# Head copies by the engines instead of DMA, and two-span projections that share one order of passes

## The chip, the cores and the metric

The kernel runs on one core of a Trainium2 chip. The metric is the time of one execution on the device in microseconds (us); lower is better. The time of a version is the median of several executions. A profile is taken from one further execution, which has its own time.

## The reference

A decoder trunk of two layers over 528 positions (16 meta tokens and 512 inputs) of width 1024. Each layer does, cut to what matters here:

```python
proj = h @ w_in[l]                    # 1024 -> 4168 columns
a, g, zc, q, k, v, za, qi, ki, wi = split(proj)
y_conv = silu(layer_norm(causal_conv31(a * sigmoid(g)))) * silu(zc)
q, k, qi, ki = rope(q), rope(k), rope(qi), rope(ki)
score = sum_h relu(qi_h . ki) * wi_h  # 8 index heads, one shared key
keep the 132 best causal keys of each query by score
y_attn = softmax(q . k on kept keys) . v * silu(za)    # 8 heads of 64
h = layer_norm(ALPHA * h + concat(y_conv, y_attn) @ w_out[l])
```

The output is h without the meta tokens. All of it is in float32 accuracy.

## The kernel before

**Layout and arithmetic.** Channels lie on the 128 partitions and positions along the free dimension. A float32 operand of a large product is split into a high part (rounded to the fp32r type, in which TensorE streams fast) and a low part (the rest). A product is then three passes over the 8 tiles of the contraction: high weight by high input, high weight by low input, low weight by high input. The input of a layer is kept as `HI` and `LO` (rows `hh` and `hl` of the profile).

**Projections.** `project(col, lo, evac)` computes one block of 128 output columns. The 528 positions don't fit one PSUM bank, so `spans` cuts them in two column spans, 0 to 272 and 272 to 528; a projection that needs at most 512 positions has one span. That holds for the four `i` jobs of each layer (396 positions, from 132 on) and, in the last layer, for the `z`, `q` and `a` jobs (512 positions, from 16 on). Of the 66 projections 46 have two spans: 29 in the first layer, 17 in the second. `product` writes the 24 matmuls of one span: 16 with the high weights, then 8 with the low weights. The PSUM tiles `acc` of the projections, `acco` of the output products and those of the `v` transposes come from one ring of three buffers (tag `acc`).

**Weights.** `weight` loads a block in two halves. For each half SyncE issues the load into `wraw` (7 buffers), ScalarE makes the high part `whi` (4 buffers) and writes a rounded copy with the opposite sign to `wlo` (5 buffers), to which the weights are then added:

```python
act.activation(h, r, AF.Copy)
act.activation(o, r, AF.Copy, scale=-1.0)
pool.dma_start(o.bitcast(F32), r, accum_op=OP.add)
```

The third line, a DMA issued by GpSimd, leaves the low part in `wlo`. TensorE can start the low pass only when that DMA has landed.

**Heads.** A block of q, k or qi columns holds two heads of 64 channels, one on each half of the partitions. `heads_q` and `heads_k` apply rope and then make one 128-partition operand for each head. For q and qi it holds the high part of the head on its own half and the low part on the other half; for k there are two, with the high part on both halves and with the low part on both halves. What must cross to the other half goes by DMA issued on SyncE. `job_kw` copies the shared index key to both halves in the same way.

**Order of the work.** All operations are recorded first. `Planner` then simulates them with prices (`_price`), latencies (`delay`) and queues, and writes each engine's program in the planned order. `ORDER` is the order of recording, `SHIFT` a table of offsets to the rank of each job, in nanoseconds. Matmuls of one `group` share one rank. The planner may put matmuls of different jobs between each other; matmuls that add into one PSUM bank stay in the order of recording. `delay` holds the planner's latency of a DMA: for one issued by GpSimd it adds 650 ns to the issue cost and the transfer. The chip's engines execute the result strictly in that order and wait on semaphores where data are late.

**Elsewhere.** `convolve` is 31 multiply-adds on VectorE for each of four channel blocks, `score` computes index scores and finds the 132 best by repeated max and replace on VectorE, `attend` does the attention, `mix` the output projection with `product` over 4 tiles, and `norm` the layer norms. Job names are those of `ORDER`: `u` (a and g), `i` (qi), `kw`, `z`, `q`, `k`, `v`, `a` (za), `s12` and `s34` (scores), `c01` and `c23` (convolution), `cl` (its layer norm), `t` (attention), `o` and `oa` (output).

Of the kernel before, what the change touches and what calls it, by code (L numbers as in the profile page):

```python
# [8 lines left out]
F32 = mybir.dt.float32  # L9
F32R = mybir.dt.float32r  # L10
BF = mybir.dt.bfloat16
AF = mybir.ActivationFunctionType
OP = mybir.AluOpType

P = 128
D = 1024
KT = D // P
# [16 lines left out]
C_KW = 32  # L34
# [10 lines left out]
)  # L45
SHIFT = {
# [21 lines left out]
}  # L68
W1 = NM + P
K_COS = 0  # L70
# [14 lines left out]
class Planner:  # L85
# [84 lines left out]

    def delay(self, a, b, true):
        if a.dma:
            far = 650.0 if a.eng == "pool" else 1950.0
            return far + a.tail + (900.0 if b.eng == "sp" else 1067.0 if b.eng == "pe" else 950.0)
        if a.eng == b.eng and (not true or a.eng == "pe"):
            return 0.0
        return self.LAT.get((a.eng, b.eng), 120) + (200.0 if (a.eng, b.eng, a.tail) == ("dve", "act", 1)
                                                    else 0.0)
# [161 lines left out]
def tile_hymba(ctx: ExitStack, tc: tile.TileContext, xt: bass.AP, wi: bass.AP, wv: bass.AP,  # L340
# [3 lines left out]
    pe, act, dve, pool, sync = (pl.engine(e) for e in ("pe", "act", "dve", "pool", "sp"))  # L344
    T = pl.tile
# [5 lines left out]
    ps = ctx.enter_context(tc.tile_pool(name="ps", bufs=1, space=bass.MemoryType.PSUM))  # L351

    HI = T(cp, [P, KT, L], F32R, name="hh")
    LO = T(cp, [P, KT, L], F32R, name="hl")
# [37 lines left out]
                w.extend(t[:, n, :] if len(t.shape) == 3 else t[:, n // 2, n % 2, :] for n in range(step))  # L392
        return W

    def product(acc, w, hi, lo, kt=KT):
        n = 0
        pl.group = len(pl.ops) + 1
        for s, m in ((w[0], hi), (w[0], lo), (w[1], hi)):
            for k in range(kt):
                pe.matmul(acc, s[k], m(k), start=(n == 0), stop=(n == 3 * kt - 1))  # L400
                n += 1
        pl.group = 0

    mean_1 = T(cp, [P, 2], F32, name="mean_c")
# [4 lines left out]
    for _ in range(SPIN):  # L409
        pe.matmul(spin[:, :2 * P], mean_c[:, 0, :], mean_1[:, 0:1].to_broadcast([P, 2 * P]), start=True,  # L410
                  stop=True)
# [31 lines left out]
    for l in range(DEPTH):  # L443
# [4 lines left out]
        def spans(lo):  # L448
            return [(lo, L)] if L - lo <= 512 else [(max(a, lo), b) for a, b in HALVES]

        def project(col, lo, evac):
            w = weight(wi[l, col], *(fresh.pop(0)() if fresh else (pool,)))
            for a, b in spans(lo):
                acc = T(ps, [P, 512], F32, name="acc", tag="acc", bufs=3)[:, :b - a]
                product(acc, w, lambda k: HI[:, k, a:b], lambda k: LO[:, k, a:b])
                evac(acc, a, b)

        def row(name, dt=F32):
            tag, n = {"xq": ("x", 2), "xk": ("x", 2), "ki": ("x", 2), "vt": ("x", 2), "rot": ("rot", 2),
                      "lq": ("lq", 2), "sg": ("sg", 1)}.get(name, ("rl", ROWS))  # L460
            return T(sp, [P, L], dt, name=name, tag=tag, bufs=n)

        def copy_to(x, scale=1.0):
            return lambda acc, a, b: act.activation(x[:, a:b], acc, AF.Copy, scale=scale)

        def rope(x, a):
            rot = row("rot")
            for g in range(2):
                sync.dma_start(rot[g::2, a:], x[1 - g::2, a:])
            dve.tensor_mul(x[:, a:], x[:, a:], cosT[:, a:])  # L470
            dve.tensor_mul(rot[:, a:], rot[:, a:], sinT[:, a:])
            dve.tensor_add(x[:, a:], x[:, a:], rot[:, a:])

        def split(x, a, hi, lo):
            act.activation(hi[:, a:], x[:, a:], AF.Copy)
            dve.tensor_tensor(lo[:, a:], x[:, a:], hi[:, a:].bitcast(F32), op=OP.subtract)

        def heads_q(col, a, keep, scale=1.0):
            x = row("xq")
            project(col, a, copy_to(x, scale))  # L480
            rope(x, a)
            s0, s1 = keep("s0"), keep("s1")
            lo = row("lq", F32R)
            split(x, a, s0, lo)
            act.activation(s1[64:, a:], x[64:, a:], AF.Copy)
            sync.dma_start(s1[:64, a:].bitcast(F32), lo[64:, a:].bitcast(F32))
            sync.dma_start(s0[64:, a:].bitcast(F32), lo[:64, a:].bitcast(F32))
            return s0, s1

        def heads_k(col, keep):  # L490
            x = row("xk")
            project(col, 0, copy_to(x))
            rope(x, 0)
            s0, s1, l0, l1 = (keep(n) for n in ("k0", "k1", "kl", "km"))
            split(x, 0, s0, l0)
            act.activation(s1[64:, :], x[64:, :], AF.Copy)
            act.activation(l1[64:, :], l0[64:, :], AF.Copy)
            for one, two in ((s0, s1), (l0, l1)):
                sync.dma_start(two[:64, :].bitcast(F32), two[64:, :].bitcast(F32))
                sync.dma_start(one[64:, :].bitcast(F32), one[:64, :].bitcast(F32))  # L500
            return (s0, s1), (l0, l1)

        def dots(qs, ks, kls, q0, m, a, b):
            out = [T(ps, [P, 512], F32, name="pl", tag="s", bufs=2)[:m, :b - a] for _ in range(2)]
# [7 lines left out]
        kw = T(sp, [P, L], F32, name="kw", tag="s01")  # L512
# [6 lines left out]

        def job_kw():  # L520
            ki = row("ki")
            project(C_KW, 0, copy_to(kw))
            for s in (0, 64):
                sync.dma_start(ki[s:s + 64, :], kw[0:64, :])
            rope(ki, 0)
            split(ki, 0, kih, kil)
            po = turn(ki, P)
            act.activation(kihr, po, AF.Copy)
            dve.tensor_tensor(kilr, po, kihr.bitcast(F32), op=OP.subtract)
# [188 lines left out]
        def keep(j):  # L718
            return lambda name: T(sp, [P, L], F32R, name=name, tag=f"{name}{j % 2}")

        def job_q(j):
            ready[j, "q"] = (heads_q(C_Q + j, qlo, keep(j), -HD ** -0.5),)

        def job_k(j):
            ready[j, "k"] = heads_k(C_K + j, keep(j))
# [9 lines left out]
        def chunks(i):  # L735
            a, b = HALVES[i]
            a = max(a, qlo)
            return a, b, [(c, min(P, b - c)) for c in range(a, b, P)]
# [77 lines left out]

        def mix(j, k0, w, hi, lo, a, b):
            acc = T(ps, [P, 512], F32, name="acco", tag="acc", bufs=3)[:, :b - a]
            product(acc, w, lambda k: hi[:, k, a:b], lambda k: lo[:, k, a:b], 4)
            r = R[j // 4][:, j % 4, a:b]  # L820
            dve.scalar_tensor_tensor(r, r, 1.0 if k0 else ALPHA, acc, op0=OP.mult, op1=OP.add)

# [35 lines left out]
        for i in range(2):  # L858
            pl.job = f"ln{i}/{l}"
            a, b, _ = chunks(i)  # L860
            norm(lambda j: R[j // 4][:, j % 4, :], KT, mean_c[:, 0, :], i, V_PG, pool, i == 1)
            for j in range(KT):
# [4 lines left out]
                else:  # L867
# [6 lines left out]
                    if not last and j % 2:  # L874
                        pool.tensor_tensor(LO[:, j, a:b], r, HI[:, j, a:b].bitcast(F32),
                                           op=OP.subtract)
# [68 lines left out]
```

## Time and profile before

| | |
|---|---|
| median of 3 executions | 675.14 us (672.87 to 675.35) |
| the profiled execution | 671.79 us |
| its span, first to last instruction | 669.8 us |
| mean granted TensorE clock, share of full speed | 0.989 |
| busy, share of the span | PE 95%, PEld 89%, DVE 78%, ACT 69%, POOL 29% |

PE are the matmuls of TensorE and PEld its weight loads, which overlap them; DVE is VectorE, ACT ScalarE, POOL GpSimd, SP SyncE, which only issues DMAs here. All instructions of this kernel are issued through one helper and so have one line number; rows are told apart by their tiles, written out<-in. A bracket at the end of a row tells how long the engine was idle before it and what ended that.

### The profile page before, as it was taken

The page shows a single profiled execution, that of the slowest core. Times are in us where ns is not written, and L with a number is a line of the kernel's source. Part 1 is how long each engine was busy: PE and PEld are TensorE (multiplying, and loading weights), DVE is VectorE, ACT ScalarE, POOL GpSimd, SP SyncE. Part 2 cuts the span into 40 slices and gives each one's busy share as a digit, 9 for nine tenths or more (in the row PEclk, how much of TensorE's full clock was granted, in tenths as well). Part 3 has the DMA queues.
Part 4 walks back from the last instruction along what each step waited for, and adds up shares of the span by engine and source line. Part 5 has one row for each costly group of instructions (what it writes and reads, how often), then busy time and mean ns, then how long its engine had stood idle before and what let it go on. Part 6 is the DMA issues. An engine that isn't in the chain of part 4 may idle for free.

```text
span 669.8 us, 13204 instructions
## 1 busy us (share of the span) xinstructions
PE 639.0 (95%) x4602; PEld 598.1 (89%) x4602; DVE 524.0 (78%) x1279; ACT 463.8 (69%) x1056; POOL 191.9 (29%) x236
## 2 busy tenths in 40 slices
PE   8999999999999998899999999999999999989993
PEld 7989999999999987899898999888999889967992
DVE  5686999999899947444563999999999999483356
ACT  7554865865756979596676665667549887895536
POOL 0423213223211322444543232223231121233262
PEclk8999999999999999899999999999999999999997
DMA  8899849748855586998315985887886783279503
GB/s 299 203 263 219 237 95 236 168 98 197 198 131 130 127 224 170 200 212 199 75 68 139 225 212 131 191 212 173 189 186 163 166 188 90 87 177 238 82 1 125
DMA packets 67570, 112.60 MB, mean 168 GB/s; under 512 B 7600, under 2 KB 21168, under 8 KB 67376
## 3 DMA queue, kind: packets, MB, share of 16 engines
q0 software_dynamic: 25088, 41.95, 37.5%
q1 hardware_dynamic: 42416, 69.81, 33.2%
q8 instruction: 36, 0.59, 0.3%
q14 instruction: 30, 0.25, 0.1%
HBM read 50.46 MB, written 4.26 MB: 82 GB/s over the span
## 4 chain that ended last, share of the span: by engine, by line
PE 56%; issue 15%; DMA 9%; DVE 6%; ACT 5%; POOL 2%; SPq 0%; POOLq 0%; ACTq 0%; DVEq 0%
PE acc L297 28%; PE acco L297 11%; DMA wlo<-wraw 5%; PE o L297 5%; PE pl L297 3%; PE pp L297 3%; PE pq L297 2%; POOL wlo L297 2%; DVE r L297 2%; DVE sc L297 1%; DMA s<-lq 1%; PE pm L297 1%; DMA kl<-kl 1%; DMA qi<-lq 1%; DMA rot<-xq 1%
## 5 line engine op out<-in xcount | busy, mean ns | idle before, releaser
L297 POOL DMA_DIRECT2D wlo<-wraw x140 | 124.0, 939 | 350.7 <-ACT wlo L297 214.1
L297 DVE SCALAR_TENSOR_TENSOR conv<-u,vec,conv 128x528 f32<-128x528 f32 (+1 forms) x240 | 176.4, 755 | 1.8
L297 PE MATMUL acc<-hh,whi 128*128 128x272 f32 (+3 forms) x872 | 154.0, 308 | 5.0 <-ACT hh L297 2.5
L297 PE MATMUL acc<-hl,whi 128*128 128x272 f32 (+3 forms) x872 | 148.1, 303 | 0.0
L297 PE MATMUL acc<-hh,wlo 128*128 128x272 f32 (+3 forms) x872 | 144.5, 304 | 3.8 <-DMA wlo<-wraw 3.5
L297 PEld LDWEIGHTS acc<-hh,whi 128*128 128x128 f32 x872 | 125.1, 190 | 11.7 <-ACT hh L297 3.9
L297 PEld LDWEIGHTS acc<-hh,wlo 128*128 128x128 f32 x872 | 123.8, 190 | 10.7 <-DMA wlo<-wraw 6.2
L297 ACT ACTIVATE whi<-wraw 128x512 fp32r<-128x512 f32 (+1 forms) x148 | 86.9, 614 | 66.3 <-PE acc L297 51.1
L297 PEld LDWEIGHTS acc<-hl,whi 128*128 128x128 f32 x872 | 124.6, 190 | 3.9 <-issue 0.2
L297 ACT ACTIVATE wlo<-wraw 128x512 fp32r<-128x512 f32 x140 | 85.5, 623 | 6.9 <-PE acc L297 4.8
L297 DVE SCALAR_TENSOR_TENSOR r<-r,acco 128x256 f32<-128x256 f32 (+2 forms) x56 | 25.8, 462 | 47.4 <-PE acco L297 47.3
L297 DVE MAX8 m<-sc 128x8 f32<-128x400 f32 (+3 forms) x106 | 55.9, 551 | 0.0
L297 DVE MATCH_REPLACE8 sc<-m,sc 128x400 f32<-128x400 f32 (+3 forms) x98 | 53.6, 549 | 0.0
L297 ACT ACTIVATE p<-p,ast 128x400 f32<-128x400 f32 (+4 forms) x72 | 40.6, 568 | 5.0 <-DVE ast L297 4.7
L297 PE MATMUL o<-v,pt 128*128 128x64 f32 x320 | 43.0, 265 | 0.5 <-ACT pt L297 0.4
L297 PEld LDWEIGHTS o<-v,pt 128*128 128x128 f32 x320 | 41.5, 192 | 1.7 <-ACT pt L297 1.1
L297 ACT ACTIVATE rl<-pl 128x272 f32<-128x272 f32 (+3 forms) x80 | 29.5, 391 | 14.8 <-PE pl L297 12.1
L297 DVE CUSTOM_DVE_ANT_0 p<-pl,bmask 128x272 f32<-128x272 f32 (+3 forms) x80 | 33.0, 433 | 7.7 <-PE pl L297 6.2
L297 ACT ACTIVATE pt<-pp 128x128 f32<-128x128 f32 (+3 forms) x64 | 26.9, 433 | 11.5 <-PE pp L297 10.7
L297 ACT ACT_TABLE_LOAD x26 | 33.4, 1283 | 1.5 <-PEq L936 0.7
L297 DVE SCALAR_TENSOR_TENSOR sc<-rl,ws,sc 12x144 f32<-12x144 f32 (+3 forms) x56 | 29.9, 555 | 0.6 <-ACT rl L297 0.3
L297 PE MATMUL pp<-konst,p 128*128 128x128 f32 x160 | 30.2, 289 | 0.0
(167 smaller groups left out, 1067.5 us busy)
## 6 DMA issues: line engine op xcount, KB each, us to landing
wlo<-wraw POOLq DMA_DIRECT2D x140, 256.0 KB, 4.9
wraw<-wi SPq DMA_DIRECT2D x128, 256.0 KB, 3.8
wraw<-wo SPq DMA_DIRECT2D x32, 256.0 KB, 4.1
hl<-wraw POOLq DMA_DIRECT2D x16, 256.0 KB, 5.2
rot<-xk SPq DMA_DIRECT2D x16, 132.0 KB, 2.7
k<-k SPq DMA_DIRECT2D x16, 132.0 KB, 3.1
r<-xt SPq DMA_DIRECT2D x2, 1056.0 KB, 8.9
r<-spill SPq DMA_DIRECT2D x2, 1024.0 KB, 6.2
```

The costliest lines, as they stand in the source:

```text
L297: self.plan.record(self.e, fn, lambda: real(*a, **k), reads, writes, *_price(self.e, fn, named, reads, writes))
```

## The change

Five edits, made together.

1. `heads_q`: for each head, ScalarE copies its 64 partitions to the high part in place, and VectorE subtracts and writes the low part straight to the other 64 partitions. Before, one ScalarE copy and one subtraction covered 128 partitions, one more ScalarE copy 64, and two DMAs moved the low parts.
2. `heads_k`: for each head three more such steps; the four DMAs are gone, and ScalarE writes the copies to the other half.
3. `job_kw`: ScalarE copies the shared index key from PSUM to both halves, instead of two DMAs.
4. `product` takes all spans of a projection at once. High weights by high and low inputs are done for the first span and then for the second, and then the low weights for the first and the second. All are one group. For one span the order is as before, in `mix` too.
5. The planner's price of a GpSimd DMA goes from 650 to 1800 ns, and the `SHIFT` table is another one. `ORDER` is the same.

```diff
 SHIFT = {
-    "a0/1": 301146, "a1/0": -624491, "a1/1": -132089, "a2/0": 1188874, "a2/1": -413625,
+    "a0/0": -21811, "a0/1": 62045, "a1/0": -1672691, "a1/1": -4829, "a2/0": -278500, "a2/1": -2793,
...
     def delay(self, a, b, true):
         if a.dma:
-            far = 650.0 if a.eng == "pool" else 1950.0
+            far = 1800.0 if a.eng == "pool" else 1950.0
...
-    def product(acc, w, hi, lo, kt=KT):
-        n = 0
+    def product(accs, w, hi, lo, spans, kt=KT):
+        count = dict.fromkeys(range(len(accs)), 0)
         pl.group = len(pl.ops) + 1
-        for s, m in ((w[0], hi), (w[0], lo), (w[1], hi)):
-            for k in range(kt):
-                pe.matmul(acc, s[k], m(k), start=(n == 0), stop=(n == 3 * kt - 1))
-                n += 1
+        for ps_ in (((w[0], hi), (w[0], lo)), ((w[1], hi),)):
+            for i, (acc, (a, b)) in enumerate(zip(accs, spans)):
+                for s, m in ps_:
+                    for k in range(kt):
+                        pe.matmul(acc, s[k], m[:, k, a:b], start=(count[i] == 0),
+                                  stop=(count[i] == 3 * kt - 1))
+                        count[i] += 1
         pl.group = 0
...
             w = weight(wi[l, col], *(fresh.pop(0)() if fresh else (pool,)))
-            for a, b in spans(lo):
-                acc = T(ps, [P, 512], F32, name="acc", tag="acc", bufs=3)[:, :b - a]
-                product(acc, w, lambda k: HI[:, k, a:b], lambda k: LO[:, k, a:b])
+            accs = [T(ps, [P, 512], F32, name="acc", tag="acc", bufs=3)[:, :b - a] for a, b in spans(lo)]
+            product(accs, w, HI, LO, spans(lo))
+            for acc, (a, b) in zip(accs, spans(lo)):
                 evac(acc, a, b)
...
-            s0, s1 = keep("s0"), keep("s1")
-            lo = row("lq", F32R)
-            split(x, a, s0, lo)
-            act.activation(s1[64:, a:], x[64:, a:], AF.Copy)
-            sync.dma_start(s1[:64, a:].bitcast(F32), lo[64:, a:].bitcast(F32))
-            sync.dma_start(s0[64:, a:].bitcast(F32), lo[:64, a:].bitcast(F32))
-            return s0, s1
+            ss = keep("s0"), keep("s1")
+            for g, t in enumerate(ss):
+                own, other = x[64 * g:64 * g + 64, a:], slice(64 - 64 * g, 128 - 64 * g)
+                hi = t[64 * g:64 * g + 64, a:]
+                act.activation(hi, own, AF.Copy)
+                dve.tensor_tensor(t[other, a:], own, hi.bitcast(F32), op=OP.subtract)
+            return ss
...
-            s0, s1, l0, l1 = (keep(n) for n in ("k0", "k1", "kl", "km"))
-            split(x, 0, s0, l0)
-            act.activation(s1[64:, :], x[64:, :], AF.Copy)
-            act.activation(l1[64:, :], l0[64:, :], AF.Copy)
-            for one, two in ((s0, s1), (l0, l1)):
-                sync.dma_start(two[:64, :].bitcast(F32), two[64:, :].bitcast(F32))
-                sync.dma_start(one[64:, :].bitcast(F32), one[:64, :].bitcast(F32))
-            return (s0, s1), (l0, l1)
+            hs, ls = [[keep(n) for n in ns] for ns in (("k0", "k1"), ("kl", "km"))]
+            for g, (h, t) in enumerate(zip(hs, ls)):
+                own, other = slice(64 * g, 64 * g + 64), slice(64 - 64 * g, 128 - 64 * g)
+                act.activation(h[own, :], x[own, :], AF.Copy)
+                dve.tensor_tensor(t[own, :], x[own, :], h[own, :].bitcast(F32), op=OP.subtract)
+                act.activation(h[other, :], x[own, :], AF.Copy)
+                act.activation(t[other, :], t[own, :].bitcast(F32), AF.Copy)
+            return hs, ls
...
-            project(C_KW, 0, copy_to(kw))
-            for s in (0, 64):
-                sync.dma_start(ki[s:s + 64, :], kw[0:64, :])
+
+            def evac(acc, a, b):
+                act.activation(kw[:, a:b], acc, AF.Copy)
+                for g in (0, 64):
+                    act.activation(ki[g:g + 64, a:b], acc[:64], AF.Copy)
+            project(C_KW, 0, evac)
...
-            product(acc, w, lambda k: hi[:, k, a:b], lambda k: lo[:, k, a:b], 4)
+            product([acc], w, hi, lo, [(a, b)], 4)
```

## Rows read from the trace of the kernel before

**Rows 1.** The page: busy time of each engine, and the DMA total.

```profile
PE 639.0 (95%) x4602; PEld 598.1 (89%) x4602; DVE 524.0 (78%) x1279; ACT 463.8 (69%) x1056; POOL 191.9 (29%) x236
...
DMA packets 67570, 112.60 MB, mean 168 GB/s; under 512 B 7600, under 2 KB 21168, under 8 KB 67376
```

**Rows 2.** Timeline, second layer: matmuls that follow each other (start, duration).

```profile
393.53 1.11 PE L297 MATMUL acc<-hh,whi 128*128 128x256 f32 x8
...
394.48 1.11 PE L297 MATMUL acc<-hl,whi 128*128 128x256 f32 x8
```

**Rows 3.** Waits of the weight loads: total us, times, longest us.

```profile
PEld acc L297 <- DMA wlo<-wraw: 6.2, 10, 1.4
PEld acco L297 <- DMA wlo<-wraw: 5.7, 2, 4.3
...
PEld pl L297 <- DMA s<-lq: 1.7, 1, 1.7
```

**Rows 4.** Timeline of the weight loads at four of the waits for wlo.

```profile
27.74 0.66 PEld L297 LDWEIGHTS acc<-hh,wlo 128*128 128x128 f32 x4 [0.80 <-DMA wlo<-wraw]
...
103.83 0.81 PEld L297 LDWEIGHTS acc<-hh,wlo 128*128 128x128 f32 x6 [0.33 <-DMA wlo<-wraw]
...
270.11 0.93 PEld L297 LDWEIGHTS acco<-ych,wlo 128*128 128x128 f32 x4 [4.34 <-DMA wlo<-wraw]
...
403.66 0.54 PEld L297 LDWEIGHTS acc<-hh,wlo 128*128 128x128 f32 x4 [1.38 <-DMA wlo<-wraw]
```

**Rows 5.** DMA issues: count, KB each, median us from issue to landing.

```profile
wlo<-wraw POOLq DMA_DIRECT2D x140, 256.0 KB, 4.9
...
k<-k SPq DMA_DIRECT2D x16, 132.0 KB, 3.1
```

**Rows 6.** Waits of the SP queue, whole span: total us, times, longest.

```profile
SPq L297 <- DMA wlo<-wraw: 222.3, 88, 6.6
...
SPq L297 <- ACT k L297: 21.4, 6, 9.5
...
SPq L297 <- DVE lq L297: 15.7, 7, 5.6
```

**Rows 7.** Timeline of the last q block of the second layer.

```profile
600.96 0.68 DVE L297 TENSOR_TENSOR lq<-xq,s 128x512 fp32r<-128x512 f32 x1
...
605.47 3.23 SPq L297 DMA_DIRECT2D s<-lq  x2
...
612.16 0.34 PE L297 MATMUL pl<-k,s 128*128 128x144 f32 x1 [1.26 <-DMA s<-lq]
```

**Rows 8.** ACT and DVE groups by form: busy us, mean ns of one | idle before.

```profile
L297 ACT ACTIVATE k<-xk 128x528 fp32r<-128x528 f32 x8 | 5.1, 643 | 1.5 <-DVE xk L297 1.5
L297 ACT ACTIVATE k<-xk 64x528 fp32r<-64x528 f32 x8 | 5.1, 643 | 0.2
...
L297 ACT ACTIVATE kw<-acc 128x272 f32<-128x272 f32 x2 | 0.8, 386 | 1.6 <-PE acc L297 1.6
...
L297 DVE TENSOR_TENSOR kl<-xk,k 128x528 fp32r<-128x528 f32 x8 | 5.6, 698 | 0.2 <-ACT k L297 0.2
...
L297 DVE TENSOR_TENSOR lq<-xq,qi 128x396 fp32r<-128x396 f32 x8 | 4.6, 570 | 3.9 <-ACT qi L297 3.8
```

**Rows 9.** Windows: busy us and count of PE, PEld, DVE, ACT, POOL; PEclk, DMA share, GB/s.

```profile
0.00:80.00 80.00, 74.78 (x507) 71.04 (x508) 58.47 (x113) 50.10 (x112) 20.61 (x30) 0.98 0.97 250
80.00:240.00 160.00, 157.79 (x1252) 152.36 (x1252) 155.97 (x381) 111.86 (x252) 37.71 (x45) 1.00 0.68 155
...
400.00:560.00 160.00, 158.19 (x1041) 143.25 (x1040) 156.30 (x377) 112.70 (x239) 38.52 (x44) 1.00 0.78 178
```

**Rows 10.** Waits of all engines: ScalarE for a free buffer of high weights.

```profile
ACT whi L297 <- PE acc L297: 51.1, 46, 5.2
```

**Rows 11.** Timeline of VectorE: two instructions of 396 columns in a row.

```profile
401.30 0.55 DVE L297 TENSOR_TENSOR xq<-xq,konst 128x396 f32<-128x396 f32 x1
401.79 0.55 DVE L297 TENSOR_TENSOR rot<-rot,konst 128x396 f32<-128x396 f32 x1
```

41 rows, old and new, of the table SHIFT are left out of this document.

## The prediction

> **What bounds the kernel now.** I read the page first. TensorE is busy for 95% of the span and no other engine for more than 78% [rows 1]. A faster kernel must therefore either give TensorE less work, which this change doesn't (it only reorders the matmuls), or take away times at which TensorE stands still. How dense the stream is when nothing is late is seen in the timeline: eight matmuls of 256 columns start 0.95 us after the eight before them, 0.119 us each [rows 2]. So nearly all of the 669.8 us is a stream that the change leaves as it is, and the prize is small.
>
> The waits of the weight loads show what holds the stream up. The low weights, which a GpSimd DMA finishes, are late ten times before projections (6.2 us) and twice before output products (5.7 us), and a q operand is late once (1.7 us) [rows 3]. That makes 13.6 us, 2.0% of the span, which the change can reach at all. The timeline of the same waits tells which edit reaches them. Five stand before two-span projections, 2.7 us together, the first 0.33 and the last 1.38 [rows 4]. Four, 3.4 us together, the first 0.80, stand before one-span projections, whose order of passes does not change, and the largest of all, 4.34, before an output product [rows 4]. The tenth before projections is some 0.1 us.
>
> Then the two engines that get more work. VectorE has 4.0 us idle between 80 and 240 us and 3.7 us between 400 and 560; ScalarE is at 70% there [rows 9].
>
> **The change, part by part.**
>
> *Low weights last.* In a two-span projection the first low matmul came behind 16 matmuls and now comes behind 32, so 16 × 0.119 = 1.9 us later [rows 2]. The longest of the five waits it concerns is 1.38 [rows 4], so each would be covered. The planner could put matmuls of other work between them before, too, so it doesn't gain more than the waits: -2.5 of the 2.7, bounds 0 and -2.7. The high weights are last read eight matmuls earlier, after 32 of 48 instead of 40, which frees ScalarE's `whi` buffers about 1 us sooner. ScalarE waits 51.1 us for those [rows 10], but it isn't the bound, and I count nothing; the cover is TensorE's own stream.
>
> *Head copies.* Gone are 68 of SyncE's DMAs: 32 for q and qi, 32 for k, 4 for the index key. One takes about 3.1 us to land [rows 5], and before that it waits in an in-order queue which stands on ScalarE's k copies for 21.4 us and on VectorE's `lq` for 15.7 [rows 6]. The last q block shows the whole path: its low part is ready at 601.64, its DMAs are issued from 605.47, and TensorE starts on it at 612.16 [rows 7]. In the new form the subtraction writes the operand itself, about 10 us sooner. TensorE stood still for only 1.7 us of that [rows 3], since output products filled the rest. Taken: -1.7, bounds 0 and -1.7. Behind these DMAs in the queue stand weight loads, but those wait mostly for a buffer, 222.3 us on the low-weight DMAs [rows 6], so I give nothing for loads that can be issued sooner. At most 68 × 132 KB = 9.0 MB of 112.6 MB traffic goes away [rows 1, 5]. Where that could count is the first 80 us, with the DMA engines 97% busy [rows 9]: 8 of the qi copies and 2 of the index key go there, at most 10 × 132 KB = 1.3 MB of 80 × 250 GB/s = 20 MB, 6.6%. If TensorE's idle 5.2 us there (80 less 74.8) were all DMA, that would give it back; taken 0, bounds 0 and -4.
>
> *What the engines get instead.* Half the partitions cost ScalarE the same, 643 ns for 64 or 128 [rows 8]. A q block keeps two copies, a k block goes from three to six: 8 × 3 × 0.643 = 15.4 us. The index key adds four copies in each layer, 8 × 0.386 = 3.1 [rows 8]. ScalarE goes from 463.8 to about 482 us, 72%, behind TensorE's stream: 0. VectorE has one more subtraction in each of 24 blocks, eight of 396 columns and sixteen of about 528: 8 × 0.570 + 16 × 0.698 = 15.7 us [rows 8], 7.9 in each layer. That lands mostly where VectorE has no room [rows 9]. What is late next is the convolution and the selection of keys, which fill that engine, and behind them the convolution's norm and the output products. The cover is attention and projection work that TensorE can take first. Without it the price is the whole 15.7. Of that, 7.7 fits into the idle time of the two full stretches, and the first layer's four qi blocks, 2.3, fall into the first 80 us, where VectorE is idle for 21.5 [rows 9]. Some 5.7 is left, and I let a third of it reach TensorE: +2.0, bounds 0 and +15.7.
>
> One rule speaks against this part. The Trainium skill, "VectorE: DVE Perf Modes", section "Two Vector instructions with no wait between them", says in a model that a VectorE instruction which starts on, or writes to, another group of 32 partitions than the one before is held until all earlier ones have finished. No row here shows that case, as all head work of before starts at the first partition; by that rule the sum would be up to 3.8 us worse, an estimate: 64 held instructions, two or three in a block, that lose the 0.06 us by which neighbours overlap. That overlap is the row's: 0.55 us long, starts 0.49 apart [rows 11].
>
> *Two accumulators open at once.* Before, a PSUM tile was filled by 24 matmuls and came into use again 48 matmuls (5.7 us) later. Now the first span's tile is complete after 40 of the 48, and the next projection's second span needs it 24 matmuls (2.9 us) on. The engine that empties it is mostly ScalarE, a 0.39 us copy [rows 8] in a queue that can stand up to 5.2 us on a weight buffer [rows 10]. TensorE would then wait. The planner knows the ring, so it can place the copies. Taken +1.0; bounds 0 and 46 projections × one matmul, 5.5.
>
> *The new plan.* The planner believed that a low-weight DMA lands sooner than it does; the row says 4.9 us from issue [rows 5]. A later price makes it issue them earlier or put other matmuls first, and so reaches the waits that the order of passes doesn't: 3.4 + 5.7 = 9.1 us [rows 3, 4]. A plan that avoids one wait moves others, and a different `SHIFT` table re-orders everything. Bounds 0 and -9.1; I take half, -4.5, as nothing in the rows puts it nearer to one end.
>
> **Sum.** -2.5 - 1.7 - 4.5 + 2.0 + 1.0 = -5.7 on the profiled execution's 671.8, so 666.1. That execution is 3.3 below the median of 675.1, so I forecast a median of 669.4 us.
>
> **Rivals.**
> - *The waits only change their place* (no change). For: the planner was already free to interleave, and TensorE's stream has hundreds of small dependences. Against: the waits named are DMAs whose lateness the plan misjudged. Gains and losses then cancel: 673 to 677.
> - *VectorE becomes the bound of the convolution* (slower). Place: 80 to 240 and 400 to 560 us, where it is idle for 4.0 and 3.7 us. It decides when TensorE runs out of other work before the convolution's norm. If the whole 15.7 arrives and the gains of 8.7 stay, it is +7.0, so 682; from 8.7 us on it is no gain any more. Against: the convolution can start earlier, in VectorE's 21.5 idle us of the first 80 [rows 9].
> - *TensorE waits for PSUM tiles* (slower). It decides where a copy is more than 2.9 us late. With one matmul's time for each of the 46, and a plan that gains nothing: 675.1 - 4.2 + 2.0 + 5.5 = 678; twice that wait, 684. For it: the buffer's spare time is halved. Against: 2.9 us is still more than seven such copies.
> - *All waits go, and the DMA relief counts* (faster): -2.7 - 1.7 - 9.1 - 4 = -17.5 without losses, so 657.6.
>
> **How the numbers follow.** Forecast (664 to 672): 0.45. Larger gain: 0.12. No change: 0.22. VectorE: 0.14. PSUM: 0.07. Half a per cent, 3.4 us, is about what a measurement of this kernel can tell from no change. So faster 0.57, same 0.22, slower 0.21. The range leaves out the end of each outer case: 659 to 680.
>
> **What the profile would show.** Right: the loads' waits for `wlo` fall from 11.9 us to under 5; no wait for `s` is left; SyncE has 68 DMAs fewer; VectorE's busy time is up by some 16 us and ScalarE's by 18; TensorE's count and pitch are as before. Wrong: new waits of TensorE for `acc` copies, or for `ych` behind a later convolution, that add up to as much as went.

## The result, and the profile after

The median went from 675.25 us (672.87 to 675.52, 4 runs) to 666.59 (663.57 to 668.84, 4 runs): 8.7 us less, ratio 0.9877 [0.9831, 0.9922]. The forecast was 669.4, with -5.7 us. The profiled executions stand at 671.79 and 663.57 us, their spans at 669.8 and 661.8, and the mean granted clock is 0.989 in both. The profiled execution is the fastest of the four after; the other three, up to 668.84 us, have mean clocks of 0.985, 0.980 and 0.976.

The page of the kernel after, busy time and DMA total (compare [rows 1]):

```profile
PE 635.7 (96%) x4602; PEld 596.9 (90%) x4602; DVE 538.7 (81%) x1303; ACT 478.6 (72%) x1086; POOL 191.6 (29%) x236
...
DMA packets 62130, 103.98 MB, mean 157 GB/s; under 512 B 6512, under 2 KB 19056, under 8 KB 61936
```

TensorE has the same 4602 matmuls. VectorE has 14.7 us more work (forecast 15.7) and ScalarE 14.8 (forecast about 18; 24 loads of function tables instead of 26, at 1.28 us each, make up most of the difference). The traffic is 8.6 MB less, where at most 9.0 was expected. The span less TensorE's busy time is the time in which it stood still: 669.8 - 639.0 = 30.8 before, 661.8 - 635.7 = 26.1 now. So 4.7 of the 8.0 us come from less idle time, and 3.3 from the same matmuls running shorter.

The waits of the weight loads after (total us, times, longest; compare [rows 3]):

```profile
PEld acc L298 <- ACT hh L298: 5.0, 9, 1.7
PEld acc L298 <- ACT xq L298: 4.6, 1, 4.6
PEld pl L298 <- ACT rl L298: 3.0, 7, 1.3
PEld pq L298 <- POOL sq L298: 1.8, 5, 0.7
PEld acc L298 <- ACT za L298: 1.7, 1, 1.7
...
PEld acc L298 <- DMA wlo<-wraw: 1.0, 2, 0.7
...
PEld acco L298 <- ACT ych L298: 0.6, 1, 0.6
```

The late low weights are down from 11.9 us to 1.0, the wait for `s` is gone, and that for `ych` fell from 2.5 us to 0.6. New are one wait of 4.6 us for an accumulator that ScalarE had not yet emptied, one of 1.7 for `za`, 1.4 us more for `rl` and 1.1 more for `hh`. So more than half of what went came back in other places.

The stretches of the span show where the time went. First the kernel after, then the two stretches of the kernel before that [rows 9] leave out (busy us and count of PE, PEld, DVE, ACT, POOL; granted clock, DMA share, GB/s):

```profile
0.00:80.00 80.00, 72.58 (x477) 68.35 (x478) 63.46 (x139) 51.04 (x114) 18.07 (x27) 0.96 0.82 216
80.00:240.00 160.00, 155.78 (x1250) 151.94 (x1248) 154.82 (x361) 114.13 (x254) 37.38 (x45) 1.00 0.67 156
240.00:400.00 160.00, 157.85 (x1214) 150.88 (x1213) 101.01 (x263) 125.63 (x303) 63.15 (x78) 1.00 0.68 158
400.00:560.00 160.00, 159.37 (x1059) 144.41 (x1058) 158.86 (x389) 119.06 (x258) 36.86 (x42) 1.00 0.66 152
560.00:662.00 102.00, 90.12 (x611) 81.28 (x609) 60.59 (x158) 68.75 (x161) 36.09 (x45) 0.96 0.50 119
```

```profile
240.00:400.00 160.00, 152.93 (x1152) 144.84 (x1151) 92.53 (x245) 116.45 (x283) 60.61 (x75) 0.99 0.72 170
...
560.00:670.00 110.00, 95.32 (x660) 86.65 (x658) 60.69 (x169) 72.66 (x174) 34.44 (x43) 0.96 0.46 111
```

Compare the counts of matmuls with those of the same stretches before. The new kernel is 30 matmuls behind at 80 us (477 against 507) and 32 at 240; it makes 62 more between 240 and 400 and 18 more between 400 and 560, and so has some 50 fewer to do at the end. Most of the gain lies in 240 to 400, where TensorE stood still for 7.1 us before and for 2.2 now; the largest wait of before, 4.34 us at 270 [rows 4], is there. The loss lies in the first 80, where the idle time rose from 5.2 us to 7.4 although the DMA share fell from 0.97 to 0.82. No gain from the relief of the DMA engines is seen there, but one new stall of 4.26 us stands in the same stretch and would hide a small one.

That stall is the place of the loss. The timeline after, around the accumulator that came late:

```profile
42.75 0.61 ACT L298 ACTIVATE whi<-wraw 128x512 fp32r<-128x512 f32 x1
43.25 0.56 DVE L298 TENSOR_TENSOR qi<-xq,qi 64x396 fp32r<-64x396 f32 x1
43.27 0.36 ACT L298 ACTIVATE kw<-acc 128x256 f32<-128x256 f32 x1
43.53 1.08 ACT L298 ACTIVATE qi<-xq 64x396 fp32r<-64x396 f32 x2
...
44.63 0.50 ACT L298 ACTIVATE xq<-acc 128x396 f32<-128x396 f32 x1
...
45.19 2.21 PE L298 MATMUL acc<-hh,whi 128*128 128x396 f32 x8 [4.26 <-ACT xq L298]
...
47.20 2.70 PE L298 MATMUL acc<-hl,whi 128*128 128x396 f32 x8
...
49.73 1.61 PE L298 MATMUL acc<-hh,wlo 128*128 128x396 f32 x8
...
51.18 1.04 PE L298 MATMUL acc<-hh,whi 128*128 128x272 f32 x7
```

The copy `xq<-acc` at 44.63 stands in ScalarE's queue behind a weight copy, a copy of the index key and two of the new 64-partition head copies. TensorE waits 4.26 us for it. Then come eight matmuls in 2.01 us (45.19 to 47.20), eight in 2.53 and eight in 1.45. The first sixteen thus cost 2.01 + 2.53 - 2 × 1.45 = 1.6 us more. The granted clock tells why. Here it is, after and then before, in the stretch that follows each kernel's longest wait of the weight loads (the last three values are granted clock, DMA share and GB/s):

```profile
46.00:50.00 4.00, 4.00 (x16) 4.00 (x15) 3.83 (x6) 2.08 (x6) 0.86 (x1) 0.57 1.01 220
```

```profile
270.20:274.00 3.80, 3.80 (x22) 3.80 (x23) 0.95 (x3) 0.00 (x0) 0.59 (x1) 0.63 1.12 206
```

In both kernels some 4 us without a matmul are followed by some 4 us in which the clock is mostly at its lower level (1.2 of 2.4 GHz). At 0.63 the 3.8 us of before give 3.8 × 0.37 = 1.4 us away, so the wait that the prediction had at 4.34 cost some 5.7.

### The profile page after: what moved, and what is told of

It is laid out like the page before. It is cut to its first block, busy times and chain, and to the rows that moved or that the text cites. A ratio compares the mean times of both kernels' runs of the same rounds, so it can differ in the third digit from the quotient of the medians.

```text
span 661.8 us, 13128 instructions
## 1 busy us (share of the span) xinstructions
PE 635.7 (96%) x4602; PEld 596.9 (90%) x4602; DVE 538.7 (81%) x1303; ACT 478.6 (72%) x1086; POOL 191.6 (29%) x236
## 3 DMA queue, kind: packets, MB, share of 16 engines
HBM read 50.46 MB, written 4.26 MB: 83 GB/s over the span
## 4 chain that ended last, share of the span: by engine, by line
PE 69%; issue 10%; DVE 9%; ACT 5%; DMA 4%; POOL 2%; SPq 0%; POOLq 0%; DVEq 0%; ACTq 0%
PE acc L298 38%; PE acco L298 14%; PE o L298 5%; PE pl L298 5%; DVE conv L298 4%; DMA wlo<-wraw 3%; PE pp L298 3%; PE pq L298 2%; POOL wlo L298 2%; DVE r L298 2%; PE pm L298 1%; DMA wraw<-wi 1%; ACT conv L298 1%; PE pmt L298 1%; ACT k L298 1%
## 5 line engine op out<-in xcount | busy, mean ns | idle before, releaser
L298 PE MATMUL acc<-hl,whi 128*128 128x272 f32 (+3 forms) x872 | 146.4, 304 | 0.0
L298 PE MATMUL acc<-hh,wlo 128*128 128x272 f32 (+3 forms) x872 | 136.6, 301 | 0.5 <-DMA wlo<-wraw 0.5
L298 PEld LDWEIGHTS acc<-hh,wlo 128*128 128x128 f32 x872 | 120.0, 188 | 4.9 <-DMA wlo<-wraw 1.0
L298 DVE MAX8 m<-sc 128x8 f32<-128x528 f32 (+3 forms) x106 | 55.8, 551 | 0.0
L298 DVE MATCH_REPLACE8 sc<-m,sc 128x528 f32<-128x528 f32 (+3 forms) x98 | 53.4, 549 | 0.0
L298 ACT ACTIVATE p<-p,ast 128x144 f32<-128x144 f32 (+4 forms) x72 | 40.6, 567 | 5.7 <-DVE ast L298 5.3
L298 ACT ACT_TABLE_LOAD x24 | 30.8, 1283 | 1.1 <-PEq L943 0.7
```

The costliest lines, as they stand in the source:

```text
L298: self.plan.record(self.e, fn, lambda: real(*a, **k), reads, writes, *_price(self.e, fn, named, reads, writes))
```

## The experiments

**Each edit alone, in the plan that is there.** Theory A: the two code edits carry the gain by the prediction's prices, and the plan the rest. Rival: the plan carries it, and an edit has no price of its own. In these four kernels the planned order is kept. In the first, the 48 matmuls of each two-span projection exchange their slots among themselves; a later instruction is moved only where a dependence asks for it.

```diff
+            if len(made) == 2:
+                m, n = made
+                TWO.append(pl.ops[m:m + 16] + pl.ops[n:n + 16] + pl.ops[m + 16:m + 24] + pl.ops[n + 16:n + 24])
...
-    order = pl.plan()
+    order = resorted(pl.plan())
```

> The kernel before with its own plan; only the matmuls of each two-span projection change places among the slots that they had, so that the low weights come last for both spans. Theory of the prediction (the order of passes is worth the waits that it covers): the waits of the weight loads for wlo fall from 11.9 us to about 9.2, the time by 2.5 us to about 672.7. Rival (the time came from the new plan, the order alone does nothing or costs PSUM waits): 674 to 678, with new waits for acc copies.

In the second, the new head and index-key copies take the places of the old ones in the old plan, and the DMAs are empty. What had no place of its own, such as the second subtraction of a q block, goes directly behind a ScalarE copy; the index key is copied from SBUF here, not from PSUM.

```diff
+            pl.ops[n].call = lambda: copy(0)
+            pl.ops[n + 1].call = lambda: low(0)
+            pl.ops[n + 2].call = lambda: (copy(1), low(1))
+            pl.ops[n + 3].call = pl.ops[n + 4].call = lambda: None
...
```

> The kernel before with its own plan; the head and index-key copies are made by ScalarE and VectorE in the places of the copies and DMAs that they replace, 68 DMAs fewer. Theory of the prediction (1.7 us of TensorE's wait go, some 2 us come back through a full VectorE): 675, within 1.5 us. Rival A (a full VectorE is the bound): VectorE's 15.7 us more arrive, 680 or more. Rival B (the DMA relief counts): the first 80 us become shorter and the time falls to 671 or less.

The third makes both edits.

> Both edits in the plan of before, so without the new price and offsets. Theory of the prediction: 675.2 - 2.5 - 1.7 + 2 = 673.0, so about a quarter of the 8.7 us that the change gave; the rest is the new plan. Rival (the two code edits carry it): 668 or less.

The fourth goes the other way: the changed kernel with its plan, but the matmuls back in the old order of passes.

```diff
+            if len(accs) == 2:
+                TWO.append(pl.ops[n:n + 16] + pl.ops[n + 32:n + 40] + pl.ops[n + 16:n + 32] + pl.ops[n + 40:n + 48])
...
-    order = pl.plan()
+    order = resorted(pl.plan())
```

> The changed kernel with its own plan; only the matmuls of each two-span projection go back to the old order of passes within their slots. Theory of the prediction: the low weights are needed 1.9 us sooner, waits for wlo come back, 2.5 us in the old plan and perhaps more here, since the plan counts on the later use: 669 to 673. Rival (the plan gives the weights enough time by itself): 666 to 668, no new wait for wlo.

Measured, against 674.52 us: 714.61 for the order alone, ratio 1.0607 [1.0567, 1.0647]; 704.32 for the heads alone, 1.0444 [1.0416, 1.0472]; 739.99 for both, 1.0956 [1.0921, 1.0990]; and 698.33, 1.0357 [1.0334, 1.0381], for the new kernel with the old passes. All four times missed what the prediction's theory expected by 25 us or more. Of the rivals only one is met by its number, that of the second kernel by which a full VectorE is the bound (680 or more). But this kernel runs in a plan made for other code, as the first does, so its number can't decide that; the kernel with the price and the heads below can. The weight loads' waits of the first and of the fourth show what went wrong (ahead of them the line of the kernel before for high weights):

```profile
PEld acc L297 <- ACT whi L297: 1.2, 2, 0.9
```

```profile
PEld acc L297 <- ACT whi L297: 8.9, 7, 3.0
PEld acc L297 <- DMA wlo<-wraw: 6.2, 7, 1.4
PEld acco L297 <- DMA wlo<-wraw: 4.6, 2, 3.0
...
PEld acc L297 <- ACT kw L297: 3.1, 2, 2.4
```

```profile
PEld acc L298 <- DMA wlo<-wraw: 21.6, 8, 5.8
PEld acc L298 <- ACT hh L298: 6.5, 8, 1.8
...
PEld acc L298 <- ACT xq L298: 4.6, 1, 4.6
```

In the first, a first span's tile is complete 16 matmuls later, and its copy stands in ScalarE's queue where the old plan put it. What is queued behind can then be late, and high weights are: 8.9 us, where it was 1.2. In the fourth, low weights that the new plan lets arrive for the end of 48 matmuls are now asked for after 16: 21.6 us, where it was 1.0. The waits alone don't make the sum. TensorE's busy time in the first is 654.4 us for the same 4602 matmuls, 15.4 more, at a mean clock of 0.977 for 0.989; its idle time is 710.2 - 654.4 = 55.8, 25 more. Stalls are paid again in slower matmuls, as at 270 us above.

So an in-order plan depends on the edit it was made for. That says nothing yet of what the edit is worth in a plan of its own.

**New plans, made alike.** For the next kernels the `SHIFT` table is searched anew from zero, by the planner's own simulated span, with about 350,000 plans for each table. First the old code with the old price, then with the edit of the price alone:

```diff
-            far = 650.0 if a.eng == "pool" else 1950.0
+            far = 1800.0 if a.eng == "pool" else 1950.0
```

> Control: code and price of before, but another table of offsets, found by a search from zero over the planner's own span (350,000 plans; every searched kernel here has the same search). It tells what a table of offsets is worth by itself. If the first runs only showed that edits in a foreign plan fail, this plan made for its code is near 675, 670 to 682. Rival (the table of before is special and any other one costs tens of us): 690 or more.

> Code of before with the price of 1800 ns for a GpSimd DMA, and offsets searched for it. Theory of the prediction (the price reaches 9.1 us of waits for wlo, half of it counted): 4 to 9 us under the control, and waits for wlo under 4 us. Rival (the price alone does nothing as long as the low weights are needed after 16 matmuls; the planner only moves other work ahead): within 2 us of the control.

Then the price with the order of passes (the new `product`, the old `heads_q`, `heads_k` and `job_kw`), and the price with the new head copies (the old `product`):

> Price and new order of passes, old head copies with their 68 DMAs, offsets searched. Theory of the prediction (the order covers 2.5 us of waits beyond the price): 2 to 4 us under the kernel with the price alone. Rival A (order and price reach the same waits): equal within 2 us. Rival B (two open accumulators make TensorE wait for PSUM): slower than the price alone, with waits for acc copies.

> Price and new head copies, old order of passes, offsets searched. Theory of the prediction (1.7 us gained, some 2 lost through VectorE): within 2 us of the kernel with the price alone. Rival A (VectorE is the bound): 4 us or more slower than it. Rival B (the path over SyncE's queue cost more than the waits that it showed): 3 us or more faster.

Measured, against 674.95 us:

| kernel | median us | ratio | planner's span |
|---|---|---|---|
| the kernel before | 674.95 | 1 | 638.3 |
| old code, old price | 668.52 | 0.9909 [0.9880, 0.9938] | 640.4 |
| price | 663.00 | 0.9829 [0.9794, 0.9864] | 637.0 |
| price and order | 662.20 | 0.9813 [0.9776, 0.9849] | 638.3 |
| price and heads | 663.34 | 0.9840 [0.9794, 0.9886] | 637.6 |

Another table for the untouched code gives 6.4 us, where the whole change gave 8.7, and the two intervals overlap. By the planner's own account this table is not even better than the one it replaced (640.4 against 638.3): with the old price the planner's span did not rank these two kernels. With the new price the gain is 12.0, without either code edit. The order then adds -0.8 and the heads +0.3, both inside the intervals. So a plan with the new price did what was expected of it (4 to 9 us under the control), the order did not (2 to 4 expected; its first rival, within 2 us, holds), and the heads did (within 2 us); that VectorE is the bound (4 us or more slower) is refuted. The control itself missed its range of 670 to 682. Theory A falls. The waits for the low weights, of the old code with the old price and with the new one:

```profile
PEld acc L288 <- DMA wlo<-wraw: 5.2, 9, 1.0
```

```profile
PEld acc L284 <- DMA wlo<-wraw: 1.4, 1, 1.4
```

With the waits before output products, 0.8 and 0.9, these sum to 6.0 and 2.3 us, where they were 11.9. The corrected price, with its table, takes most of them away without a new order of passes.

**All edits, with a table of the same kind.** Theory B: the edits help together where each alone does not. Rival: the shipped table was merely a weaker one. Two searches with different random numbers, and a third in which the planner is told that instructions on 64 partitions take longer, as the trace after shows (below):

```diff
-        c += 93 * (a.get("accum_out") is not None)
+        c += 93 * (a.get("accum_out") is not None) + 125 * (writes[0].shape[0] == 64)
...
+        c += 112 * (writes[0].shape[0] == 64)
```

> Code and price of the changed kernel, offsets searched as in the four runs before instead of the table that came with the change. Theory after those runs (price 5.5 us, order 0.8, heads nothing): 662 to 664, so also 3 to 4 us under the changed kernel's 666.6, whose table then was not the best for it. Rival (the two code edits help each other, since the order needs the freed queue): 658 or less.

> The same with another seed of the search (its planned span is within 0.1 us of the first). Tells how far two equally good tables lie apart on the chip: within 2 us if differences of that size between the searched kernels mean something; rival: 4 us or more apart, and then nothing under that can be put down to an edit.

> As the first, with one more price: the planner is told that an instruction of ScalarE or VectorE on 64 partitions costs 125 or 112 ns more, which is what the trace of the changed kernel shows they lose by not overlapping their neighbours. Theory (these instructions make both engines late against the plan, and this is what the head copies cost): 1 to 4 us faster than without. Rival (both engines have slack for it): within 1 us of it.

Measured, against 673.39 us: 659.05, ratio 0.9782 [0.9744, 0.9821]; 659.55, 0.9799 [0.9745, 0.9854]; and 662.79, 0.9834 [0.9797, 0.9870]. The first two are about 1% faster than the shipped table with the same code, by the ratios, though the intervals of the second and of the shipped kernel still overlap. The planner agrees: it gives the shipped table, with the new price, a span of 640.4 us and these two 631.7. So the shipped table was the weaker one. The times lie between theory (662 to 664) and rival (658 or less) of the first, and the two are 0.5 us apart, within the 2 expected. The third did not improve on them, though a gain of 1 to 4 us was expected: a copy of `xq` out of PSUM is late again, for 5.5 us, and the high inputs `hh` are late for 6.5 in all:

```profile
PEld acc L293 <- ACT hh L293: 6.5, 7, 1.8
PEld acc L293 <- ACT xq L293: 5.5, 1, 5.5
```

So telling the planner of the held instructions, although they are real, gave no better kernel in this one search.

**The control for the plan's quality.** The first two have a planner's span of 631.7 us, and the price alone had one of 637.0. Either the edits make the better plans possible, or the search with the price alone had been unlucky. Another search of the old code with the new price, from another seed, ended at 631.3, and its kernel was run:

> Code of before with the new price again, but a table from another seed, whose planned span (631.3 us) is that of the two kernels with all edits (631.7), not 637.0 as in the first run with the price alone. Theory (the two code edits give some 3 us beyond the price): 661 to 664, ratio about 0.983. Rival (at equal planned span they give nothing, and the 4 us between the price alone and all edits were the luck of the search): 657 to 660, ratio about 0.979.

Measured: 659.84 us against 674.56, ratio 0.9775 [0.9756, 0.9794]. That is the same as all edits with a plan of equal length (0.9782 and 0.9799). The page of this kernel, with the old code:

```profile
PE 635.1 (96%) x4602; PEld 598.3 (91%) x4602; DVE 521.5 (79%) x1279; ACT 456.1 (69%) x1050; POOL 191.8 (29%) x236
...
DMA packets 67570, 112.60 MB, mean 171 GB/s; under 512 B 7600, under 2 KB 21168, under 8 KB 67376
```

VectorE has 17 us less work than in the changed kernel and the DMA engines 8.6 MB more, and the time is that of the versions with all edits. The rival stands: it expected 657 to 660, and theory 661 to 664. Over the kernels with the new price, with or without the edits (the third search aside, as it had other prices), the time goes with the planner's span: 659 to 660 us at 631.3 to 631.7, 662 to 664 at 637.0 to 638.3, and 666.6 at 640.4, the shipped table. The weight loads' largest waits of this kernel, and then of the first one with all edits:

```profile
PEld acc L295 <- ACT hh L295: 4.6, 5, 1.6
PEld acco L295 <- DMA wlo<-wraw: 2.8, 3, 1.7
...
PEld acc L295 <- ACT xq L295: 2.0, 2, 1.5
PEld acc L295 <- DMA wlo<-wraw: 1.8, 3, 0.8
```

```profile
PEld acc L294 <- ACT hh L294: 4.8, 7, 1.6
PEld acc L294 <- ACT xq L294: 2.0, 1, 2.0
PEld pq L294 <- POOL sq L294: 1.6, 4, 0.7
```

The waits for `hh` and `xq` are in both. What the edits do achieve is seen there too: with all of them no wait for `wlo` is left among the largest, and with the old code 2.8 + 1.8 = 4.6 us are. Yet the two kernels take the same time.

## Why the prediction was right, and which step was mis-sized

*The total.* -5.7 was forecast and -8.7 measured, inside the likeliest case (664 to 672). The signs came as told: `wlo` 11.9 to 1.0 us, `s` gone, 8.6 MB less traffic, VectorE +14.7, the count of matmuls as before. The pitch of the matmuls is unchanged too, 0.95 us for eight matmuls of 256 columns as in [rows 2]:

```profile
396.82 1.11 PE L298 MATMUL acc<-hh,whi 128*128 128x256 f32 x8
397.77 0.40 PE L298 MATMUL acc<-hl,whi 128*128 128x256 f32 x2
```

That the total came out near is in part luck. The prediction could not know how good the shipped table is, and with better tables the same edits gave -14.3 and -13.8, over twice the forecast. The prediction's sign of being wrong, new waits for copies out of the accumulators, came too, if not in full: 4.6 us for `xq` and 1.7 for `za`.

*Low weights last, -2.5.* That the order covers late low weights fits the waits: with the new price and the new order 0.6 us of them are left, with the old order 2.3 and 4.6 in the two tables of the old code. The value did not come out. With equal treatment of the plans the order is worth -0.8 us, which can't be told from nothing; the fourth kernel's 32 us are what the plan depends on, not what the edit earns.

*Head copies, -1.7, and VectorE's extra work, +2.0.* Together +0.3 was forecast, and the price with the heads stands at +0.3 against the price alone. That the two agree to the tenth is chance, since two tables of one code lie 3.2 us apart (below). The extra work found its cover: of the 14.7 us, 5.0 went into the first 80 us (58.47 to 63.46) and 8.5 into 240 to 400 (92.53 to 101.01), and only 1.4 into the two stretches where VectorE is full. The prediction had let all but 2.3 fall into those two stretches, of which 5.7 found no idle time. VectorE did not become the bound.

*Two accumulators open at once, +1.0.* One late copy out of PSUM costs 4.3 us and some 1.6 of slow clock behind it. That is more than the value taken, and slightly above the upper bound of 5.5. It is not the mechanism that was priced: the late tile belongs to a one-span `i` job, and the copy stands behind others in ScalarE's queue. The fourth experiment bears this out: with the old order of passes in the same plan the wait for `xq` is 4.6 us as well, and with the price and the new order, in a plan of their own, the longest is 1.2. That another queue order would mend it in the shipped kernel was not tried by itself. The stretch of 46 to 50 us is at full clock in the last kernel, whose plan has no such stall there:

```profile
46.00:50.00 4.00, 4.00 (x32) 4.00 (x31) 3.82 (x6) 2.12 (x4) 1.74 (x2) 1.00 1.09 260
```

*The new plan, -4.5, bounds 0 and -9.1.* This is the mis-sized step. A table alone gave 6.4 us, and price and table, with none of the code edits, 12.0 and 14.7. The bound was wrong in kind. It summed the waits of TensorE that a late low weight ends, but a new table moves every wait, and a long wait carries its slow clock too. For the same reason the 13.6 us that the prediction gives as what the change can reach at all are no limit: up to 14.7 were reached.

*The rule of the Trainium skill* ("VectorE: DVE Perf Modes", section "Two Vector instructions with no wait between them") was weighed ahead of the result and no row of before showed its case. The trace after does on VectorE. ScalarE, of which that section says nothing, shows the like in the second view:

```profile
117.71 0.69 DVE L298 TENSOR_TENSOR kl<-xk,k 64x528 fp32r<-64x528 f32 x1
118.44 0.70 DVE L298 TENSOR_TENSOR km<-xk,k 64x528 fp32r<-64x528 f32 x1
119.17 1.44 DVE L298 TENSOR_TENSOR s<-xq,s 64x528 fp32r<-64x528 f32 x2
```

```profile
119.50 0.64 ACT L298 ACTIVATE kl<-kl 64x528 fp32r<-64x528 f32 x1
120.17 0.64 ACT L298 ACTIVATE km<-km 64x528 fp32r<-64x528 f32 x1
120.72 0.63 ACT L298 ACTIVATE rl<-pl 128x256 f32<-128x256 f32 x2
```

Each VectorE instruction that changes halves starts 0.03 us behind the end of the one before, where neighbours overlapped by 0.06 [rows 11]. So the rule agrees with the trace, at 0.09 us for each and not 0.06 (0.11 against the median overlap of neighbours in the whole trace, 0.08, which is the 112 ns that the third search charged). For 64 of them that is 5.8 us of VectorE's time, an estimate. The time of the kernel does not show it: the heads cost +0.3 in all.

*What stays open.* How much of the gain belongs to the price and how much to luck with the table: the two tables of the old code with the new price lie 3.2 us apart (663.00 and 659.84), and the old price was run with one new table only. What each edit contributes inside the shipped table can't be told, since neither can be taken out of it without breaking it.

## What to carry to other kernels

Where a kernel's order is planned ahead and its engines run it strictly, value an edit only with a plan made anew for it, beside the old code planned anew with the same effort; here that control, with one price corrected, took 2.2% off. Correct first the planner's price of the operation that the trace shows landing late; here the corrected price was worth 5.5 us between two tables searched alike, with up to 3.2 us of that open to luck. And don't take the sum of the waits as the limit of what a new plan can gain: a stall of 4 us is paid again in slow matmuls behind it.

## What the runs showed of the hardware

- A stall of TensorE of 4.1 to 4.3 us was followed by some 4 us at a granted clock of 0.57 and 0.63, 1.4 to 1.6 us lost on top.
- ScalarE loses its overlap too when it changes halves: copies of 64x528 start 0.67 us apart at a length of 0.64, and so 0.03 behind the end of the one before, while the next ordinary instruction (120.72) starts 0.09 ahead of that end. It is the change of half and not the width: over the whole trace after, 64-partition copies that stay in the half of the 128-partition instruction before them (both start at partition 0) overlap it by 0.10 us in the median, and those that change it start 0.02 behind its end, and so do those of the kernel before, which all start at partition 64. The 125 ns that the third search charged for them are this 0.10 and 0.02.
- A kernel whose plan doesn't fit loses clock as well: the mean fell from 0.989 to 0.977, 0.964 and 0.954 in the first three experiments.
- A lower DMA share in the first 80 us brought no visible time. In the two kernels with all edits and new tables it is 0.88 and 0.90, and TensorE stands still there for 5.7 us in each; in the last kernel, with the old code, it is 0.98, and TensorE stands still for 4.9.
